# A fused backbone step on one core: the attention's TensorE order written out by hand, with pieces of the gate and q blocks between its products

## The chip, the cores and the metric

The kernel runs on one core of a Trainium2 chip. The core has a matrix engine (TensorE, PE in the profile), a vector engine (DVE), a scalar engine (ACT), a general one (POOL), and a queue engine that issues most transfers (SP). Each works through its own list of instructions in order and waits on semaphores for the others. The metric is the device time of one execution in microseconds (us), lower is better.

## The reference, cut to what matters

One layer of a hybrid backbone over 1024 latent and 128 context tokens, width 1024. One input projection gives the columns of a Fourier mixer, of q (16 heads of 64), k and v (4 kv heads) and of two gates. The part that is changed is the attention with what lies beside it.

```python
def attend_block(qb, k_all, v_all, sink, mask):
    scores = jnp.einsum('btkgd,blkd->bkgtl', qb, k_all,
                        preferred_element_type=jnp.float32) * (HEAD_DIM ** -0.5)
    if mask is not None:
        scores = jnp.where(mask[None, None, None], scores, NEG_INF)
    sink_col = jnp.broadcast_to(sink.astype(jnp.float32).reshape(N_KV_HEADS, Q_PER_KV)[None, :, :, None, None],
                                scores.shape[:-1] + (1,))
    p = jax.nn.softmax(jnp.concatenate([scores, sink_col], axis=-1), axis=-1)[..., :-1]
    return jnp.einsum('bkgtl,blkd->btkgd', p.astype(v_all.dtype), v_all)
...
def merge_branches(u_f, attn_o, g, w_fo, w_ao, w_out):
    gates = jax.nn.sigmoid(g)
    g_f, g_a = gates[..., :D_MODEL], gates[..., D_MODEL:]
    m = g_f * (fourier_mix(u_f) @ w_fo) + g_a * (attn_o @ w_ao)
    return m @ w_out
```

A block of 128 queries sees up to three blocks of 128 latent keys and the 128 cached context keys; the context tokens see only themselves.

## The kernel before

All activations are kept transposed (channels on the 128 partitions). Every matrix product of the input projection is done in three parts with a value split in a high and a low half (`mm3`: high x high, high x low, low x high). The normed input `hs` lies in SBUF (tiles BR and BT) until the last block of q and gate columns is done.

The stages in order: modulation and norm; the Fourier columns and the Fourier mixer, with gate blocks as filler; q of the first kv group; k and v of all nine token tiles (two rounds, PSUM tiles `x`); five gate blocks more (`FILL_KV`); the attention; the Fourier projection `f_unit`; gates, output projection, and the MLP.

A *gate block* (`gate_units`) is 128 gate columns by a third of the tokens (384): 24 products of 384 columns into a PSUM tile `mm`, a copy to `z` by ACT, a store to `z_d`. Three of them share one weight tile, which is loaded (`wraw`), and split by ACT (`whi`, L147) and DVE (`wlo`, L142). A *q block* (`q_units`) has the same 24 products; DVE applies the rotary tables (`qt`, L619 to L625), ACT and DVE split the result, and it is stored to `q_d`. There are 48 gate blocks and 24 q blocks.

The attention runs over 36 *units*, 4 kv groups by 9 query blocks (8 latent ones, one of context). Each has 4 heads and `nb` key blocks (3 at the rims, 4 inside, 1 for context). In `attention_scores`, for each head, two products (L726, L727) put the scores in a PSUM tile `s`, of which there are three. DVE adds the mask, and takes the maximum with the sink logit in the same instruction (L728, result `pt`, maximum `mx`). When a pair of heads has its two maxima, a small DVE instruction multiplies both by -0.125 (L738). Then ACT takes the exponential of each head with that as bias (L740), DVE the reciprocal of the two sums (L748), and POOL scales `pt` (L750). `attention_out` works one unit later: for each pair of heads and two key blocks, PE transposes four 128 x 128 blocks of `pt` into a PSUM tile `ptp` (L769, two buffers), ACT and DVE split it into `ph` and `pl` (L774, L142), and two products of 256 columns per key block (L779, L780) add up the values in a PSUM tile `o`, of which there is one. ACT and DVE add the two halves up (`ot`, `at`) and it is stored to `att_d`. `put_k` transposes the keys of the next group (L805).

Beside the attention run 50 blocks, 18 of q for the next groups and 32 of gates (list `work`, spread over 34 units by `fill`), and 100 steps of the second part of the modulation (`mod_step`: a load `mraw`, two ACT products `mprod`, a POOL sum `macc`, L305 and L307), queued behind POOL's scaling.

What sets the order: the program is traced in the order of the code, and a scheduler at compile time then lays down each engine's list, with the order of the code as priority and a model of its own of how long things take. `issue_after` ties a filler block to the scores of its unit. The order of PE's products within the attention is therefore the scheduler's.

## Time and profile before

| | |
|---|---|
| median of 3 runs (lowest to highest) | 1735.53 us (1731.82 to 1736.85) |
| the profiled execution's own time | 1734.79 us |
| its span, first to last instruction | 1733.0 us |
| granted TensorE clock, mean | 0.986 |
| busy share PE / PEld / DVE / ACT / POOL | 95% / 84% / 67% / 52% / 16% |
| last product of k and v (L235) | 252.1 us |
| first score (L726) / first score of unit 34 of 0 to 35 | 277.0 us / 734.3 us |
| first product of `f_unit` (L880) / of the output projection (L1145) | 741.1 us / 892.5 us |

Times inside the profile are microseconds from the first instruction. PE rows are matrix products, PEld the loads of their stationary operand. Products are pipelined, so a row's duration is longer than the distance to the next one: what a product costs is the distance from start to start. In a group's row stand the busy time and the mean of one instruction in ns, then the engine's idle time just ahead of them, and who ended it.

### The profile page before, as it was taken

To read this page: it belongs to the slowest core of one execution; us is meant where nothing else is said; L and a number is where in the kernel's file an instruction comes from. 1 tells how busy PE (TensorE), PEld (TensorE's weight loads), DVE (VectorE), ACT (ScalarE), POOL (GpSimd) and SP (SyncE) were. 2 spreads that over 40 slices of the span, in tenths; PEclk is the share of its full clock that TensorE was granted. 3 is DMA by queue.
4 is the path that set the end of the run, shared out by engine and by line. 5 is a ranking of instruction groups with operands and counts; after the bars stand their busy time and mean duration, and the time that the engine had idled before them with its cause. 6 is when DMAs were issued, how large, how long until landed. Compare 5 with 4: busy or idle time off the path is not lost.

```text
span 1733.0 us, 25745 instructions
## 1 busy us (share of the span) xinstructions
PE 1640.6 (95%) x8669; PEld 1448.6 (84%) x8669; DVE 1163.2 (67%) x2334; ACT 906.6 (52%) x1826; POOL 272.2 (16%) x368
## 2 busy tenths in 40 slices
PE   6999998789889899999999989999999999999998
PEld 5899887688778888989998788888888888888887
DVE  6653344656856776777856886777776588877764
ACT  7733124566666677766435664444444354444542
POOL 1010013444444445420001210000000200000000
PEclk9999999899999999999999999999999999999999
DMA  8442447324345343249755524454446897556751
GB/s 294 131 145 76 146 150 169 123 77 122 107 107 129 104 120 91 74 141 317 252 174 191 186 98 155 167 171 164 157 145 144 277 384 242 193 186 193 238 176 61
DMA packets 220100, 284.93 MB, mean 164 GB/s; under 512 B 30952, under 2 KB 147624, under 8 KB 219840
## 3 DMA queue, kind: packets, MB, share of 16 engines
q1 hardware_dynamic: 211712, 273.33, 49.5%
q0 software_dynamic: 8256, 9.96, 2.4%
q8 instruction: 68, 1.11, 0.3%
q14 instruction: 64, 0.52, 0.1%
HBM read 205.34 MB, written 77.88 MB: 163 GB/s over the span
## 4 chain that ended last, share of the span: by engine, by line
PE 67%; DVE 8%; DMA 3%; ACT 3%; issue 3%; POOL 1%; SPq 0%; DVEq 0%; ACTq 0%; POOLq 0%
PE x L1711 6%; PE x L1710 6%; PE x L1712 6%; PE x L1314 6%; PE x L1316 6%; PE x L1315 6%; PE mm L195 3%; PE mm L196 3%; PE mm L197 3%; PE x L196 2%; PE x L195 2%; PE x L197 2%; PE ptp L769 2%; DVE pt L728 2%; PE x L1147 1%
## 5 line engine op out<-in xcount | busy, mean ns | idle before, releaser
L142 DVE TENSOR_TENSOR wlo<-wraw,whi 128x1024 fp32r<-128x1024 f32 x108 | 139.3, 1291 | 100.5 <-ACT whi L147 99.5
L147 ACT CAST whi<-wraw 128x1024 fp32r<-128x1024 f32 x106 | 110.8, 1049 | 109.3 <-PE x L235 23.5
L196 PE MATMUL mm<-BR,whi 128*128 128x384 f32 x408 | 140.5, 344 | 0.0
L1711 PE MATMUL x<-BR 128*128 128x512 f32 (+1 forms) x348 | 132.8, 382 | 0.0
L1712 PE MATMUL x<-BR 128*128 128x512 f32 (+1 forms) x348 | 132.4, 382 | 0.0
L1710 PE MATMUL x<-BR 128*128 128x512 f32 (+1 forms) x348 | 131.1, 382 | 0.0
L195 PE MATMUL mm<-BR,whi 128*128 128x384 f32 x360 | 125.2, 348 | 2.4 <-DVE qt L619 2.1
L740 ACT ACTIVATE pt<-pt,mx 128x513 f32<-128x513 f32 (+2 forms) x144 | 94.5, 658 | 58.0 <-DVE mx L738 55.9
L197 PE MATMUL mm<-BR,wlo 128*128 128x384 f32 x360 | 124.0, 344 | 0.0
L750 POOL TENSOR_SCALAR pt<-pt,mx 128x512 f32<-128x512 f32 (+2 forms) x144 | 93.6, 662 | 184.7 <-DVE mx L748 179.0
L728 DVE CUSTOM_DVE_ANT_0 pt<-s,mask,sink 128x512 f32<-128x512 f32 (+2 forms) x144 | 93.1, 673 | 39.3 <-PE ptp L769 33.4
L1683 ACT CAST BR<-aa 128x512 fp32r<-128x512 f32 x80 | 49.7, 621 | 105.2 <-PE x L1711 46.8
L307 POOL TENSOR_TENSOR macc<-macc,mprod 128x512 f32<-128x512 f32 x70 | 92.7, 1325 | 29.9 <-ACT mprod L305 29.8
L142 DVE TENSOR_TENSOR pl<-ptp,ph 128x512 fp32r<-128x512 f32 (+1 forms) x136 | 84.7, 639 | 17.3 <-ACT ph L774 16.0
L726 PE MATMUL s<-kth,qT 128*128 128x512 f32 (+2 forms) x144 | 60.8, 424 | 32.8 <-DVE mx L728 31.0
L769 PE MATMUL ptp<-ident,pt 128*128 128x128 f32 x496 | 74.6, 278 | 10.6 <-DVE pl L142 8.2
L1314 PE MATMUL x<-BR,whi 128*128 128x512 f32 (+2 forms) x204 | 79.2, 388 | 4.1 <-ACT ZR L1338 2.8
L196 PEld LDWEIGHTS mm<-BR,whi 128*128 128x128 f32 x408 | 79.5, 195 | 1.3
L774 ACT CAST ph<-ptp 128x512 fp32r<-128x512 f32 (+1 forms) x136 | 70.9, 547 | 15.1 <-PE ptp L769 12.0
L779 PE MATMUL o<-ph,vg 128*128 128x256 f32 x248 | 68.0, 296 | 10.9 <-DVE at L786 6.2
L305 ACT ACTIVATE mprod<-mraw,siluc 128x256 f32<-128x256 f32 x140 | 63.7, 503 | 27.5 <-POOL macc L307 22.4
L1316 PE MATMUL x<-BR,wlo 128*128 128x512 f32 (+2 forms) x204 | 77.6, 380 | 0.0
(450 smaller groups left out, 4885.6 us busy)
## 6 DMA issues: line engine op xcount, KB each, us to landing
aa<-hr_d SPq DMA_DIRECT2D x108, 256.0 KB
ab<-in_w_ff_dram SPq DMA_DIRECT2D x108, 256.0 KB
hr_d<-ZR SPq DMA_DIRECT2D x104, 256.0 KB
wraw<-in_w_in_dram SPq DMA_DIRECT2D x40, 512.0 KB
wraw<-in_w_ff_dram SPq DMA_DIRECT2D x34, 512.0 KB
mraw<-in_w_ada_dram SPq DMA_DIRECT2D x96, 128.0 KB
wraw<-in_w_out_dram SPq DMA_DIRECT2D x24, 512.0 KB
z_d<-z SPq DMA_DIRECT2D x48, 192.0 KB
```

Source lines behind the costliest of these rows:

```text
L142: eng.tensor_tensor(dst, raw, hi.bitcast(F32), ALU.subtract)
L147: nc.scalar.copy(hi, raw)
L195: nc.tensor.matmul(out, ah, bh, start=start, stop=False)
L196: nc.tensor.matmul(out, ah, bl, start=False, stop=False)
L197: return nc.tensor.matmul(out, al, bh, start=False, stop=stop).ins
L728: nc.vector.tensor_tensor_reduce(out=pt[:, e, :n], in0=sp[:, :n], in1=mask[:, m0 : m0 + n], scale=1.0, scalar=sink8[:, h0 + e : h0 + e + 1 ...
L769: nc.tensor.transpose(pst[:, bi, e, :], pt[:, e, b * P : (b + 1) * P], ident)
L1314: nc.tensor.matmul(po, wh, xh, start=(k == 0 and not cont), stop=False, skip_group_check=cont)
L1316: nc.tensor.matmul(po, wl, xh, start=False, stop=(k == 3), skip_group_check=cont)
L1710: nc.tensor.matmul(ps, xh, bh, start=start, stop=False, skip_group_check=cont)
L1711: nc.tensor.matmul(ps, xh, bl, start=False, stop=False, skip_group_check=cont)
L1712: nc.tensor.matmul(ps, xl, bh, start=False, stop=stop, skip_group_check=cont)
```

## The change

The four parts, as the diff has them:

- **Order.** From unit 0 to 33, PE's list is kept in the order of the code (`manual_schedule` for PE alone); the other engines' lists stay the scheduler's. A q or gate block becomes a generator that hands over after each `mm3` (8 pieces a block). `gap()` is called between the products of the attention and lets so many pieces through that the 440 pieces of 55 blocks are spread evenly by `weight`. A unit then has four scores with a piece or two between them, and after that, for the unit before, transposes and value products in turn: the values of a key block come one key block after its transposes.
- **What stands where.** The five gate blocks behind k and v (`FILL_KV`) go into the attention, and the q blocks of the first group take their place (they stood ahead of k and v).
- **Negative scores.** The DVE instruction that adds the mask multiplies by -0.125 as well and takes the minimum with the negative sink logit; the exponential has scale -1 and that minimum as bias. L738 is gone, and the exponential of a head no longer stands behind the other head of its pair.
- **Four heads at once.** A `ptp` tile holds one key block of four heads (before: two key blocks of two heads); a value product has 512 columns (before: 256), `o` serves four heads, and `ot` and `at` are twice as wide and half as many.

`z` gets three buffers, `ra` and `rb` of k and v one. The diff, cut to what is spoken of:

```diff
-FILL_KV = 5
-FILL_AT = 34
...
+        ZB[0] = 3
...
+        nsink = p1.tile([P, 16], F32, name="nsink")
+        nc.vector.tensor_scalar(nsink, sink_sb, -1.0, None, ALU.mult)
...
+            def piece(j, e):
+                blk = wcols(fetch(ws[e]), KC)
+                ps = mmt()
+                r = slice(j * CH, (j + 1) * CH)
+                v = ps[:, :CH]
+                for k in range(KC):
+                    mm3(v, *blk[k], hs[k][0][:, r], hs[k][1][:, r], k == 0, k == KC - 1)
+                    if k < KC - 1:
+                        yield
...
+        def gate_piece(m, j, w):
+            blk = wcols(fetch(w), KC)
+            ps = mmt()
+            r = slice(j * CH, (j + 1) * CH)
+            for k in range(KC):
+                mm3(ps[:, :CH], *blk[k], hs[k][0][:, r], hs[k][1][:, r], k == 0, k == KC - 1)
+                if k < KC - 1:
+                    yield
+            z = p1.tile([P, CH], F32, tag="z", name=nm("z"), bufs=ZB[0])
+            nc.scalar.copy(z, ps[:, :CH])
+            nc.sync.dma_start(z_d[m][:, j * CH : (j + 1) * CH], z)
...
-            anchor = tok_proj_round(ROUNDS[1], OFF_KV, bankk, evac_kv)
-            filler(FILL_KV, anchor)
+            tok_proj_round(ROUNDS[1], OFF_KV, bankk, evac_kv)
+            for piece in q_pieces(0):
+                for _ in piece:
+                    pass
...
+        def score_head(u, h):
+            g, i, qT = u["g"], u["i"], u["q"]
             k0, nb = KWIN[i]
             n = nb * P
             m0 = MWIN[i] * P
+            pr, e = h // 2, h % 2
+            h0 = g * 4 + pr * 2
+            if e == 0:
+                pt = p1.tile([P, 2, 516], F32, tag="pt", name=nm("pt"), bufs=4)
+                mx = p1.tile([P, 6], F32, tag="mx", name=nm("mx"), bufs=4)
+                u["pts"].append(pt)
+                u["mx"] = mx
+                nc.gpsimd.tensor_copy(pt[:, :, n : n + 1], nsink[:, h0 : h0 + 2].unsqueeze(2))
+            pt, mx = u["pts"][-1], u["mx"]
+            sp = q1.tile([P, 512], F32, tag="s", name=nm("s"), bufs=3)
+            qs = qT[:, h, (i % 3) * P : (i % 3 + 1) * P]
+            nc.tensor.matmul(sp[:, :n], qs, kth[:, k0 * P : k0 * P + n], start=True, stop=False)
+            nc.tensor.matmul(sp[:, :n], qs, ktl[:, k0 * P : k0 * P + n], start=False, stop=True)
+            nc.vector.tensor_tensor_reduce(
+                out=pt[:, e, :n],
+                in0=sp[:, :n],
+                in1=mask[:, m0 : m0 + n],
+                scale=-0.125,
+                scalar=nsink[:, h0 + e : h0 + e + 1],
+                op0=ALU.add,
+                op1=ALU.min,
+                accum_out=mx[:, e : e + 1],
+            )
+            nc.scalar.activation(
+                pt[:, e, : n + 1],
+                pt[:, e, : n + 1],
+                AF.Exp,
+                bias=mx[:, e : e + 1],
+                scale=-1.0,
+                accum_out=mx[:, 2 + e : 3 + e],
+            )
+            if e == 0:
+                return
+            nc.vector.reciprocal(mx[:, 4:6], mx[:, 2:4])
+            for e in range(2):
+                ins = nc.gpsimd.tensor_scalar(
+                    pt[:, e, :n], pt[:, e, :n], mx[:, 4 + e : 5 + e], 1.0, ALU.mult, ALU.mult
+                )
+            if len(msteps) > MOD_B:
+                with tc.issue_after(ins.ins):
+                    mod_step(min(MOD_A[pr], len(msteps) - MOD_B))
+
+        def out_t(u, b):
+            pst = q1.tile([P, 512], F32, tag="ptp", name=nm("ptp"), bufs=2)
+            for h in range(4):
+                nc.tensor.transpose(pst[:, h * P : (h + 1) * P], u["pts"][h // 2][:, h % 2, b * P : (b + 1) * P], ident)
+            ph = p1.tile([P, 512], F32R, tag="ph", name=nm("ph"), bufs=3)
+            pl = p1.tile([P, 512], F32R, tag="pl", name=nm("pl"), bufs=3)
+            nc.scalar.copy(ph, pst)
+            sub(nc.vector, pl, pst, ph)
+            u["p"][b] = ph, pl
+
+        def out_v(u, b):
+            k0, nb = KWIN[u["i"]]
+            if b == 0:
+                u["o"] = q1.tile([P, 512], F32, tag="o", name=nm("o"), bufs=1)
+            po = u["o"]
+            ph, pl = u["p"].pop(b)
+            kb = {"c": 9, "x": 8}.get(KT_ORDER[k0 + b], KT_ORDER[k0 + b])
+            vst = u["v"][:, kb].rearrange("p a d -> p (a d)")
+            nc.tensor.matmul(po, vst, ph, start=(b == 0), stop=False)
+            nc.tensor.matmul(po, vst, pl, start=False, stop=(b == nb - 1))
+            if b < nb - 1:
+                return
+            ot = p1.tile([P, 2, P], F32, tag="ot", name=nm("ot"), bufs=2)
+            at = p1.tile([P, 2, P], F32, tag="at", name=nm("at"), bufs=2)
+            pv = po.rearrange("p (r e t) -> p e r t", r=2, e=2)
+            for e in range(2):
+                top, bot = slice(64 * e, 64 * e + 64), slice(64 - 64 * e, 128 - 64 * e)
+                nc.scalar.copy(ot[top], pv[bot, e])
+                nc.vector.tensor_tensor(at[top], pv[top, e], ot[top], ALU.add)
+            g, i = u["g"], u["i"]
...
-                nc.vector.tensor_scalar(mx[:, 2:4], mx[:, 0:2], -0.125, None, ALU.mult)
...
-                        nc.tensor.matmul(po[:, :256], vst, ph[:, bi, :], start=(b == 0), stop=False)
-                        nc.tensor.matmul(po[:, :256], vst, pl[:, bi, :], start=False, stop=(b == nb - 1))
...
-        def fill(s, after):
-            left = total - min(total, -(-total * s // FILL_AT))
-            with tc.issue_after(after):
-                while len(work) > left:
-                    work.pop(0)()
...
+        def fill_steps():
+            for pc, b, q in pieces_:
+                for w in blocks_[: b + 2]:
+                    fetch(w)
+                for _ in pc:
+                    yield
+                if q is not None:
+                    qdone.add(q)
+                yield
+
+        steps_ = fill_steps()
+
+        def fill_to(x):
+            while done[0] < min(NSUB, round(x)):
+                next(steps_, None)
+                done[0] += 1
+
+        def weight(s):
+            cur = KWIN[units[s][1]][1]
+            prev = KWIN[units[s - 1][1]][1] if s else 0
+            return cur + prev
+
+        NMAN = len(units) - 2
+        wsum = sum(weight(s) for s in range(NMAN))
...
+        man = ExitStack()
+        man.enter_context(tc.manual_schedule(engines={mybir.EngineType.PE}))
+        base, pending = 0.0, None
+        for s in range(NMAN):
+            u = begin(s)
+            nb = KWIN[pending["i"]][1] if pending else 0
+            spots = 4 + (2 * nb + 1 if pending else 0)
+            share = NSUB * weight(s) / wsum
+            seen = [0]
+
+            def gap():
+                seen[0] += 1
+                fill_to(base + share * seen[0] / spots)
+
+            for h in range(4):
+                score_head(u, h)
+                gap()
+            for b in range(nb):
+                out_t(pending, b)
+                gap()
+                if b:
+                    out_v(pending, b - 1)
+                gap()
+            if nb:
+                gap()
+                out_v(pending, nb - 1)
+            base += share
+            fill_to(base)
+            next_keys(*units[s])
+            pending = u
+        fill_to(NSUB)
+        for _ in steps_:
+            pass
+        man.close()
+        for s in range(NMAN, len(units)):
+            u = begin(s)
+            for h in range(4):
+                score_head(u, h)
+            nb = KWIN[pending["i"]][1]
+            for b in range(nb):
+                out_t(pending, b)
+                out_v(pending, b)
+            pending = u
+            if s == NMAN:
+                load_fx()
+            f_unit(NF)```

PE's list at the unit of group 1, query block 4 (unit 13), before. `s` are its scores, `ptp` and `o` the transposes and the values of the unit before it, `mm` a q or gate block.

```order
L726 MATMUL s_4511<-kth,qT_3846 128x512
L727 MATMUL s_4511<-ktl,qT_3846 128x512
L769 MATMUL ptp_4402<-ident,pt_4141 128x128 x4
L726 MATMUL s_4515<-kth,qT_3846 128x512
...
L726 MATMUL s_4536<-kth,qT_3846 128x512
...
L779 MATMUL o_4238<-ph_4244,vg_2722 128x256
L780 MATMUL o_4238<-pl_4245,vg_2722 128x256
...
L769 MATMUL ptp_4415<-ident,pt_4141 128x128 x4
L769 MATMUL ptp_4436<-ident,pt_4170 128x128 x4
L726 MATMUL s_4540<-kth,qT_3846 128x512
L727 MATMUL s_4540<-ktl,qT_3846 128x512
L195 MATMUL mm_4631<-BR,whi_4108 128x384
```

Four scores, three groups of transposes and eight value products stand together there, and the 24 products of a block follow in one piece. The same unit in the changed kernel:

```order
L752 MATMUL s_4234<-kth,qT_3633 128x512
L753 MATMUL s_4234<-ktl,qT_3633 128x512
L193 MATMUL mm_4197<-BR,whi_3479 128x384
...
L752 MATMUL s_4242<-kth,qT_3633 128x512
...
L752 MATMUL s_4279<-kth,qT_3633 128x512
L753 MATMUL s_4279<-ktl,qT_3633 128x512
L193 MATMUL mm_4293<-BR,whi_3828 128x384
...
L786 MATMUL ptp_4297<-ident,pt_4065 128x128 x2
L786 MATMUL ptp_4297<-ident,pt_4099 128x128 x2
L193 MATMUL mm_4293<-BR,whi_3828 128x384
```

A piece of three products (of which only the first is shown) stands between any two scores and behind each group of transposes. In short, with `f` for a piece, `T` and `V` for the four transposes and the two value products of a key block, the unit reads: s f s f s f f s f T f f T f V f T f V f f T f V f f V.

DVE's list from the last score of the same unit on, in the changed kernel; `qt` and `wlo` belong to the q and gate blocks, `pl` is what the value products wait for.

```order
L754 ISA pt_4261,mx_4262<-s_4279,mask,nsink 128x512
...
L140 TENSOR_TENSOR wlo_4376<-wraw_4373,whi_4375 128x1024
L140 TENSOR_TENSOR pl_4303<-ptp_4297,ph_4302 128x512
...
L140 TENSOR_TENSOR pl_4318<-ptp_4312,ph_4317 128x512
L140 TENSOR_TENSOR pl_4336<-ptp_4330,ph_4335 128x512
L633 TENSOR_TENSOR qt_4350<-mm_4293,ropet 128x384
L634 TENSOR_TENSOR qt_4352<-mm_4293,ropet 128x384
L635 TENSOR_TENSOR qt_4275<-qt_4275,qt_4350 128x384
L636 TENSOR_TENSOR qt_4277<-qt_4277,qt_4352 128x384
L140 TENSOR_TENSOR wlo_4658<-wraw_4655,whi_4657 128x1024
L140 TENSOR_TENSOR pl_4370<-ptp_4364,ph_4369 128x512
```

Two weight splits and the evacuation of a q block stand ahead of the first and of the last `pl` of the unit. In the unit after it the scheduler has the four in a row:

```order
L754 ISA pt_4442,mx_4443<-s_4453,mask,nsink 128x512
...
L774 RECIPROCAL mx_4409<-mx_4409 128x2
L774 RECIPROCAL mx_4443<-mx_4443 128x2
L140 TENSOR_TENSOR pl_4482<-ptp_4476,ph_4481 128x512
L140 TENSOR_TENSOR pl_4498<-ptp_4492,ph_4497 128x512
L140 TENSOR_TENSOR pl_4516<-ptp_4510,ph_4515 128x512
L140 TENSOR_TENSOR pl_4533<-ptp_4527,ph_4532 128x512
L811 TENSOR_TENSOR at_4557<-o_4504,ot_4556 64x256
```

Neither list gives a time; it only says what stands behind what.

More of the change, by code (lines that the diff above doesn't have):

```diff
@@ L488, in backbone_kernel @@
         gates = list(gate_units())
+        gate_ids = [(m, j) for m in range(16) for j in range(NJ)]
         def filler(n, after=None):
@@ new lines, in q_pieces, with tile_ @@
+        def q_pieces(g, ws=None):
+            ws = ws or q_weights(g)
+            t = {}
+            tt = nc.vector.tensor_tensor
+            def tile_(n):
+                t[n] = p1.tile([P, CH], F32, tag=f"qt{n}", name=nm("qt"), bufs=1)
+                return t[n]
+            def piece(j, e):
[7 more added lines that the diff above has]
+                        yield
+                c, sn = ropet[:, 0, r], ropet[:, 1, r]
+                if e == 0:
+                    tt(tile_(0), v, c, ALU.mult)
+                    tt(tile_(1), v, sn, ALU.mult)
+                    return
+                tt(tile_(2), v, sn, ALU.mult)
+                tt(tile_(3), v, c, ALU.mult)
+                tt(t[0], t[0], t[2], ALU.subtract)
+                tt(t[1], t[1], t[3], ALU.add)
+                for n in range(2):
+                    hi, lo = t[2 + n].bitcast(F32R), t[n].bitcast(F32R)
+                    nc.scalar.copy(hi, t[n])
+                    sub(nc.vector, lo, t[n], hi)
+                    nc.sync.dma_start(q_d[g, j, n], t[2 + n])
+                    nc.sync.dma_start(q_d[g, j, 2 + n], t[n])
@@ L633, in q_units @@
[L633 to L636 removed]
+                    yield piece(j, e)
+        def gate_piece(m, j, w):
[9 more added lines that the diff above has]
+            nc.sync.dma_start(z_d[m][:, j * CH : (j + 1) * CH], z)
@@ L912, in backbone_kernel @@
             put_k(kv[0][0], q)
-        work, qdone = [], {0: True}
-        def q_last(g, f):
-            f()
-            qdone[g] = True
-        share = -(-len(gates) // NG)
+        blocks_, pieces_ = [], []
+        gate_left = gate_ids[48 - len(gates) :]
+        share = -(-len(gate_left) // NG)
+        gw = {}
         for g in range(NG):
             if g + 1 < NG:
-                fs = list(q_units(g + 1))
-                work += fs[:-1] + [lambda g=g + 1, f=fs[-1]: q_last(g, f)]
-            for _ in range(min(share, len(gates))):
-                work.append(gates.pop(0))
@@ L926, in backbone_kernel @@
-        total = len(work)
-        def fill(s, after):
-            left = total - min(total, -(-total * s // FILL_AT))
-            with tc.issue_after(after):
-                while len(work) > left:
-                    work.pop(0)()
+                ws = q_weights(g + 1)
+                for n, pc in enumerate(q_pieces(g + 1, ws)):
+                    pieces_.append((pc, len(blocks_) + n % 2, g + 1 if n == 5 else None))
+                blocks_ += ws
+            for _ in range(min(share, len(gate_left))):
+                m, j = gate_left.pop(0)
+                if m not in gw:
+                    gw[m] = (OFF_GF + m * P, {}), len(blocks_)
+                    blocks_.append(gw[m][0])
+                pieces_.append((gate_piece(m, j, gw[m][0]), gw[m][1], None))
@@ L961, in backbone_kernel @@
         f_unit(NF2)
-        attention_out(*pending)
+        for b in range(KWIN[8][1]):
+            out_t(pending, b)
+            out_v(pending, b)
     q3 = ctx.enter_context(tc.tile_pool(name="q3", bufs=6, space=PSUM))
```

136 lines of the change are left out of this document (21 added, 115 removed).

## The prediction

> **What bounds the kernel now.** I read the time by stage first, cut where PE's work changes, then who waits for whom in the long stage, then PE's own timeline there.
>
> ```profile
> span 1733.0 us, 25745 instructions
> 171.00:186.00 15.00, 12.92 (x72) 12.61 (x71) 2.72 (x7) 2.84 (x8) 0.84 (x5) 0.96 0.52 189
> 252.00:277.00 25.00, 23.12 (x136) 22.27 (x134) 9.00 (x14) 7.33 (x15) 3.84 (x5) 1.00 1.05 234
> 277.00:734.30 457.30, 402.30 (x2400) 374.31 (x2401) 309.11 (x837) 298.07 (x755) 199.40 (x274) 0.96 0.38 105
> 734.30:892.50 158.20, 155.70 (x926) 150.23 (x925) 123.04 (x263) 85.94 (x186) 13.87 (x29) 0.99 0.70 223
> ```
>
> Columns: length, then busy time of PE, PEld, DVE, ACT and POOL, granted clock, DMA share, GB/s. The attention (fourth row, units 0 to 33) is the place: PE stands idle for 55.0 of 457.3 us, its clock is 0.96, and DVE (309) and ACT (298) are busy for two thirds only. So no engine is full; PE waits on latencies. The row after it is full (155.7 of 158.2).
>
> ```profile
> PEld s L726 <- DVE mx L728: 42.2, 42, 5.1
> PE s L726 <- DVE mx L728: 31.0, 32, 4.8
> ACT pt L740 <- DVE mx L738: 54.2, 36, 4.2
> PE ptp L769 <- DVE pl L142: 8.2, 7, 3.4
> PEld o L780 <- DVE pl L142: 5.2, 10, 1.2
> ACT macc L305 <- DMA mraw<-in_w_ada_dram: 7.5, 5, 3.5
> ```
>
> Most of PE's idle time (31.0) is a score that wants one of the three `s` tiles back from DVE. ACT waits 54.2 us for the small L738. Such a gap costs twice:
>
> ```profile
> 505.00 0.63 PE L769 MATMUL ptp<-ident,pt 128*128 128x128 f32 x4 [1.93 <-DVE pl L142]
> 506.98 0.69 PE L726 MATMUL s<-kth,qT 128*128 128x384 f32 x1 [1.35 <-DVE mx L728]
> ...
> 511.95 0.52 PE L196 MATMUL mm<-BR,whi 128*128 128x384 f32 x1
> 512.27 0.47 PE L197 MATMUL mm<-BR,wlo 128*128 128x384 f32 x1
> ```
>
> After two gaps of 1.93 and 1.35 us the products of 384 columns start 0.32 us apart until 512.27, where 0.17 is usual (below). [...]
>
> **What the same work costs without waits.** Distances from start to start:
>
> ```profile
> 520.86 0.33 PE L195 MATMUL mm<-BR,whi 128*128 128x384 f32 x1
> ...
> 523.80 0.34 PE L197 MATMUL mm<-BT,wlo 128*128 128x384 f32 x1
> ...
> 251.17 0.39 PE L234 MATMUL x<-wlo,BT 128*128 128x512 f32 x1
> 251.40 0.39 PE L235 MATMUL x<-whi,BT 128*128 128x512 f32 x1
> ...
> 517.42 0.28 PE L780 MATMUL o<-pl,vg 128*128 128x256 f32 x1
> 517.54 0.28 PE L779 MATMUL o<-ph,vg 128*128 128x256 f32 x1
> ...
> 525.43 0.87 PE ptp L769 x8
> ```
>
> 17 steps in 2.94 us are 0.173 for 384 columns; 0.228 for 512 (0.23 here); 0.119 for 256 (0.12); 0.109 for a transpose. The counts, by tile, `mm`, `ptp`, `o` and `s` in turn (18 of the `mm` are small ones of the modulation):
>
> ```profile
> 277.00:734.30 457.30, 229.35 (x1194) 214.03 (x1194) 24.43 (x72) 14.79 (x31) 0.96 0.38 105
> 277.00:734.30 457.30, 72.66 (x488) 58.12 (x488) 83.60 (x134) 70.27 (x134) 0.96 0.38 105
> 277.00:734.30 457.30, 77.35 (x445) 65.00 (x445) 36.01 (x126) 32.80 (x126) 0.96 0.38 105
> 277.00:734.30 457.30, 83.49 (x273) 47.29 (x274) 90.80 (x138) 0.00 (x0) 0.96 0.38 105
> ```
>
> 1176 x 0.173 + 2 = 206, 488 x 0.109 = 53, 445 x 0.119 = 53, and 273 scores (192 of 512 columns, the others 384 and 128) 56: together 368 us. So this stage loses 457 - 368 = **89 us**, 55 of them idle and some 18 by the clock (4% of 457). By the same count 252 to 277 holds five blocks (120 x 0.173 = 20.8) and 1.3 us of key transposes and loses 2.9, and at 184.4 the first q block waits for its rotary table:
>
> ```profile
> 184.44 0.44 PE L195 MATMUL mm<-BR,whi 128*128 128x384 f32 x1 [2.08 <-DVE qt L619]
> ```
>
> With the half clock after it, that is 3.9. **Lost before the tail: 96 us.** The work stays the same; what counts is how much of the 96 is lost again.
>
> **The change part by part.**
>
> *Four heads at once* saves PE 2 x 0.119 - 0.228 = 0.01 us a product pair, 0.02 a key block with two pairs: 2.3 us over 116 blocks. The transposes stay as many.
>
> *q of group 0 behind k and v*: the wait for the rotary table goes (3.9), since k and v need no table until their evacuation; the five blocks' cover of the evacuation is replaced by six q blocks (25 us). New there: the first unit reads q back right after it was stored.
>
> ```profile
> 264.87 9.06 DMA qT<-q_d
> ...
> 305.24 4.58 DMA q_d<-qt
> ```
>
> The chain of waits (start, length) has such a load at 9.1 and a store at 4.6 us; the first third is ready 8.3 us into the 25, so it is hidden with some 3 us to spare. I take 0, range 0 to 5.
>
> *Negative scores* remove 68 of these on DVE and let each exponential follow its own minimum:
>
> ```profile
> L738 DVE TENSOR_SCALAR mx<-mx 128x2 f32<-128x2 f32 x68 | 17.5, 258 | 0.3
> L728 DVE CUSTOM_DVE_ANT_0 pt<-s,mask,sink 128x512 f32<-128x512 f32 x96 | 69.2, 746 | 12.2 <-PE ptp L769 11.3
> L142 DVE TENSOR_TENSOR pl<-ptp,ph 128x512 fp32r<-128x512 f32 x103 | 68.9, 686 | 15.0 <-ACT ph L774 14.2
> L142 DVE TENSOR_TENSOR wlo<-wraw,whi 128x1024 fp32r<-128x1024 f32 x15 | 22.9, 1526 | 8.0 <-ACT whi L147 7.0 <-PE ptp L769 0.8
> L619 DVE TENSOR_TENSOR qt<-mm,ropet 128x384 f32<-128x384 f32 x18 | 9.6, 555 | 8.7 <-DMA q_d<-qt 4.7 <-PE mm L197 2.7 <-PE o L780 1.2
> L624 DVE TENSOR_TENSOR qt<-qt,qt 128x384 f32<-128x384 f32 x9 | 7.2, 797 | 0.0
> L740 ACT ACTIVATE pt<-pt,mx 128x513 f32<-128x513 f32 x96 | 68.7, 717 | 41.3 <-DVE mx L738 40.7 <-POOL pt L721 0.4
> L740 ACT ACTIVATION_READ_ACCUMULATOR pt<-pt,mx 128x1 f32 x136 | 25.4, 187 | 0.0
> L774 ACT CAST ph<-ptp 128x512 fp32r<-128x512 f32 x103 | 57.9, 584 | 13.0 <-PE ptp L769 10.4 <-PE o L779 1.6
> ```
>
> DVE's 17.5 us and ACT's waits lie off the sum: neither engine is full. The minimum in place of the maximum is not in the trace; the nearest row is L728 itself, 746 ns, and I take that.
>
> *The order* is the big term. The scores' wait goes: a piece of 3 x 0.173 = 0.52 stands between scores of 0.46, so one comes each 0.98 us where L728 takes 0.75, and there are three tiles. What is late next is `pl`. From a key block's transposes to its values the list leaves 2.0 to 2.5 us (two pieces, other transposes 0.44, a piece, often values 0.46). The chain is the cast (0.58), the subtraction (0.69) and three hand-overs of about 0.15, 1.7 us: enough, if both engines are free. Anything ahead of them in their lists is a wait of PE, and all pieces stand behind it.
>
> I walked four units with these durations. Unit 13, whose DVE list the section on the change shows, is a bad one. From its first score at 0: fourth score at 3.4, DVE busy with `qt` until 4.8, L728 to 5.5, `wlo` (1.53) to 7.2, the first `pl` at 7.9; the second value product wanted it at 7.1: **0.8** lost. After the third `pl`, two of L633's kind (0.56 each, once the block's last product is done at 11.3), two of L635's (0.80), `wlo` again, and the last `pl` ends at 16.2 against 13.8: **2.4**. Unit 14, four `pl` in a row, loses 0.7, since an exponential and a copy stand ahead of the first cast on ACT; units 20 and 21 lose 0.3 and 1.2 (21 evacuates a q block). Mean 1.25 by 34 units is 43; weighed by kind (nine units evacuate a q block, 2.2 each; 25 others 0.5; 19 weight splits, some 0.4) 40. I take **40**. The range is wide: from 10, where queues happen to be clear, to 90, where each of 116 blocks waits 0.8.
>
> *The rest*: first and last units, where nothing is pending or the scheduler's order returns, 3 each; casts behind ACT's waits for the modulation's loads (7.5 before) 4; half clock 5, since the largest gap that I walked, 2.4 us, is shorter than the 3.3 above. [...]
>
> Lost again: 40 + 6 + 4 + 5 = **55**. The span becomes 1733 - 96 - 2 + 55 = 1690. The profiled execution took 1734.79, 1.8 more than its span, and 0.7 less than the median of 1735.5: **1693 us** against that median.
>
> **The rivals.**
>
> *PE runs almost without waits* (the queues of DVE and ACT clear before each `pl`): 15 to 20 us lost in all, 1653 to 1658. For it: DVE (309, less 17.5, and an estimated 20 for the five blocks that move in) and ACT (298 and the same) would be busy for some 310 to 320 of its 400 us. Against it: the list above, where 1.5 to 4 us of other work stand ahead of a `pl`.
>
> *The fixed order gives most of it back*: about 85 lost, 1712 to 1735. That takes a mean of 0.6 to 0.8 us a block.
>
> *Slower: each value product waits behind a full queue.* Place: `ph` on ACT behind an exponential (0.72 and 0.19 for its read of the sum), `pl` on DVE behind an L728 (0.75). The chain is then 1.7 + 0.9 + 0.75 = 3.4 against 2.0 to 2.5 us, 1.1 late, 116 x 1.1 = 128; with the 15 of the rest 143 lost, and the time is 1781. It decides from 0.7 us a block on: 116 x 0.7 + 15 = 96, where nothing is won. The row PEld `o` <- DVE `pl` (10 waits, 5.2 us, half a microsecond each) speaks against it as the rule, and shows that it occurs. [...]
>
> *It doesn't do what it says*: the minimum runs slower than the maximum. At twice 0.75 DVE gets 136 x 0.6 = 80 us more, is nearly full, and PE follows it: about 1740.
>
> **How the numbers follow.** Forecast (1675 to 1711) 0.56, almost no waits 0.17, most given back 0.13, slower 0.10, slow minimum 0.04. 0.3% of the median, about what a measurement can tell from no change, is 5 us: below 1730.3 counts as faster. That takes the forecast, the second and two thirds of the third: 0.82; the same 0.06; slower 0.12. The range reaches from 1653 (the second's end) to 1731 (most of the third); it leaves out some 0.03 below and 0.16 above.
>
> **What would show it.** Right: the scores' wait for DVE falls from 31.0 to under 8 us; the waits of `o` for `pl` and `ph` rise from under 20 to about 40 and become PE's largest; the granted clock of the stage is 0.98 or more; unit 0 to 34 takes some 445 us with 55 blocks in it, and ACT no longer waits for L738. Wrong: PE idle over 80 us in the stage; L728's successor above 0.85 us; a gap of over 5 us ahead of the first score, where q is read back.

## The result, and the profile after

The changed kernel takes **1685.66 us** (median of 4 runs, 1682.73 to 1687.13), the kernel before 1735.59 (1731.82 to 1736.85): a ratio of 0.971, with a 95% interval of 0.969 to 0.973. The forecast was 1693. The profiled execution has a span of 1685.2 us and took 1687.13.

The stages are cut at the same places as before: end of k and v at 225.3, first score at 256.0, first score of unit 34 at 683.9. The attention of the changed kernel between the last two, with the columns as in the prediction:

```profile
256.00:683.90 427.90, 408.53 (x2309) 371.16 (x2308) 289.97 (x705) 295.08 (x693) 194.87 (x274) 0.99 0.44 119
```

It takes 427.9 us where it took 457.3, with five blocks more in it, at a clock of 0.99. I count what was lost as in the prediction: each product by its distance start to start (0.228, 0.174, 0.119 and 0.110 us for 512, 384, 256 and 128 columns), and the stage's length less their sum. Before, the products come to 369.4 us and 87.9 are lost; now to 389.4, and 38.5 are lost. The whole difference of the spans, 1733.0 - 1685.2 = 47.8, is: 49.4 less lost in this stage; 2.4 less work by wider value products; as much lost ahead of it as before, to within 0.2; and 4.3 more lost behind it.

The waits of the same stretch (who waits for whom: us in total, times, longest):

```profile
PEld o L802 <- DVE pl L140: 19.9, 32, 2.3
ACT macc L303 <- DMA mraw<-in_w_ada_dram: 11.9, 7, 4.7
PEld o L801 <- ACT ph L789: 11.8, 10, 5.3
PE o L802 <- DVE pl L140: 8.8, 19, 1.9
PE o L801 <- ACT ph L789: 8.6, 8, 5.0
PE ptp L786 <- POOL pt L776: 0.9, 2, 0.7
PEld s L752 <- DVE mx L754: 0.2, 1, 0.2
```

The scores' wait for DVE, 31.0 us before, is gone (the last row, 0.2 us, is of a weight load; the products themselves have none). What PE still waits for is `pl` and `ph`: 17.4 us as products, 26.4 by the distances from start to start. The longest of these comes from a load. This is the chain of waits (start, length):

```profile
460.02 6.68 DMA mraw<-in_w_ada_dram
466.78 0.70 ACT macc L303 x2
...
470.28 0.48 ACT ph L789
470.80 0.80 PE o L801
```

ACT's list has a product of the modulation ahead of three exponentials (a row `pt` counts each with its read of the sum) and the cast; its load lands late, all of them stand, and PE waits 5.2 us for one value product.

Unit 13, walked in the prediction, shows the ordinary case. DVE's and then PE's timeline at its last key block:

```profile
427.78 0.56 DVE L633 TENSOR_TENSOR qt<-mm,ropet 128x384 f32<-128x384 f32 x1 [0.67 <-PE mm L195]
...
428.72 0.55 DVE L635 TENSOR_TENSOR qt<-qt,qt 128x384 f32<-128x384 f32 x1
429.19 0.55 DVE L636 TENSOR_TENSOR qt<-qt,qt 128x384 f32<-128x384 f32 x1
429.66 1.22 DVE L140 TENSOR_TENSOR wlo<-wraw,whi 128x1024 fp32r<-128x1024 f32 x1
430.79 0.68 DVE L140 TENSOR_TENSOR pl<-ptp,ph 128x512 fp32r<-128x512 f32 x1
```

```profile
427.58 0.60 PE L786 MATMUL ptp<-ident,pt 128*128 128x128 f32 x4
...
430.06 0.40 PE L801 MATMUL o<-ph,vg 128*128 128x512 f32 x1
431.53 0.51 PE L802 MATMUL o<-pl,vg 128*128 128x512 f32 x1 [1.08 <-DVE pl L140]
```

It is the list that was foreseen: evacuation of a q block and a weight split ahead of the last `pl`, and 1.08 us of idle PE (1.25 by the distances) where 2.4 had been worked out.

### The profile page after: what moved, and what is told of

Read it like the earlier page. It is cut to its first block, busy times and chain, and to the rows that moved or that the text cites. A ratio compares the mean times of both kernels' runs of the same rounds, so it can differ in the third digit from the quotient of the medians.

```text
span 1685.2 us, 24900 instructions
## 1 busy us (share of the span) xinstructions
PE 1624.9 (96%) x8421; PEld 1422.9 (84%) x8421; DVE 1137.1 (67%) x2179; ACT 897.0 (53%) x1743; POOL 268.2 (16%) x368
## 3 DMA queue, kind: packets, MB, share of 16 engines
q8 instruction: 66, 1.08, 0.3%
## 4 chain that ended last, share of the span: by engine, by line
PE 64%; DVE 9%; DMA 4%; ACT 4%; issue 3%; POOL 2%; SPq 0%; DVEq 0%; ACTq 0%; POOLq 0%
PE x L1806 6%; PE x L1807 6%; PE x L1805 6%; PE x L1409 6%; PE x L1411 6%; PE x L1410 6%; PE mm L193 3%; PE mm L195 3%; PE mm L194 3%; PE ptp L786 2%; DVE pt L754 2%; PE o L802 2%; PE x L194 1%; PE x L195 1%; PE x L193 1%
## 5 line engine op out<-in xcount | busy, mean ns | idle before, releaser
L140 DVE TENSOR_TENSOR wlo<-wraw,whi 128x1024 fp32r<-128x1024 f32 x109 | 138.4, 1272 | 94.7 <-ACT whi L145 94.7
L193 PE MATMUL mm<-BR,whi 128*128 128x384 f32 x360 | 129.5, 360 | 0.3 <-DVE mods L272 0.3
L140 DVE TENSOR_TENSOR pl<-ptp,ph 128x512 fp32r<-128x512 f32 x124 | 84.7, 687 | 65.2 <-ACT ph L789 64.7
L776 POOL TENSOR_SCALAR pt<-pt,mx 128x512 f32<-128x512 f32 (+2 forms) x144 | 94.7, 670 | 206.3 <-DVE mx L774 204.2
L195 PE MATMUL mm<-BR,wlo 128*128 128x384 f32 x360 | 122.9, 341 | 0.0
L754 DVE CUSTOM_DVE_ANT_0 pt<-s,mask,nsink 128x512 f32<-128x512 f32 (+2 forms) x144 | 94.5, 670 | 14.3 <-PE s L753 11.6
L789 ACT CAST ph<-ptp 128x512 fp32r<-128x512 f32 x124 | 70.9, 578 | 41.7 <-PE ptp L786 37.2
L1409 PE MATMUL x<-BR,whi 128*128 128x512 f32 (+2 forms) x204 | 79.6, 390 | 4.1 <-ACT ZR L1433 2.8
L1410 PE MATMUL x<-BR,whi 128*128 128x512 f32 (+2 forms) x204 | 78.0, 382 | 0.0
L193 PE MATMUL mm<-BT,whi 128*128 128x384 f32 x216 | 77.1, 357 | 0.0
L140 DVE TENSOR_TENSOR BR<-aa,BR 128x512 fp32r<-128x512 f32 x80 | 55.2, 690 | 32.4 <-ACT BR L1778 31.5
L786 PE MATMUL ptp<-ident,pt 128*128 128x128 f32 x496 | 75.1, 274 | 1.8 <-POOL pt L776 0.9
```

The costliest lines, as they stand in the source:

```text
L140: eng.tensor_tensor(dst, raw, hi.bitcast(F32), ALU.subtract)
L193: nc.tensor.matmul(out, ah, bh, start=start, stop=False)
L195: return nc.tensor.matmul(out, al, bh, start=False, stop=stop).ins
L754: nc.vector.tensor_tensor_reduce(out=pt[:, e, :n], in0=sp[:, :n], in1=mask[:, m0 : m0 + n], scale=-0.125, scalar=nsink[:, h0 + e : h0 + e ...
L1409: nc.tensor.matmul(po, wh, xh, start=(k == 0 and not cont), stop=False, skip_group_check=cont)
L1410: nc.tensor.matmul(po, wh, xl, start=False, stop=False, skip_group_check=cont)
```

## The experiments

All times are medians of 4 runs (the fifth row: one run); ratios are against the kernel before on the same chip. "Lost" is the attention's length less its products' own time, as above.

| kernel | time, us | ratio (95%) | attention, us | lost there |
|---|---|---|---|---|
| before | 1735.59 | | 457.3 | 87.9 |
| the change | 1685.66 | 0.971 (0.969 to 0.973) | 427.9 | 38.5 |
| e1: change, order left to the scheduler | 1659.56 | 0.957 (0.954 to 0.961) | 411.0 | 14.5 |
| e2: change, positive maximum | 1704.16 | 0.982 (0.980 to 0.985) | 444.5 | 55.3 |
| e5: change, whole blocks | 1763.53 | (1 run) | 506.5 | 117.8 |
| e3: change, values two key blocks behind | 1685.70 | 0.971 (0.968 to 0.974) | 426.1 | 36.2 |
| g3: change, scores spread | 1698.75 | 0.981 (0.978 to 0.983) | 446.7 | 52.7 |
| h2: change, another written order | 1666.55 | 0.962 (0.960 to 0.964) | 418.4 | 28.2 |
| f1: e1 with positive maximum | 1678.66 | 0.968 (0.966 to 0.970) | 424.5 | 29.6 |
| f2: e1 with whole blocks | 1659.66 | 0.956 (0.954 to 0.958) | 407.5 | 15.3 |
| f3: e1 with values for two heads | 1671.93 | 0.963 (0.961 to 0.965) | 415.2 | 16.5 |
| g5: e1, filling whole behind the last score | 1672.65 | 0.965 (0.964 to 0.967) | 424.2 | 28.8 |
| g1: e1 with q first, five gate blocks behind k and v | 1680.46 | 0.970 (0.968 to 0.972) | 413.4 | 34.8 |
| f4: before with negative scores | 1714.98 | 0.989 (0.987 to 0.990) | 434.2 | 65.4 |

### The written order taken away (e1)

```diff
-        man.enter_context(tc.manual_schedule(engines={mybir.EngineType.PE}))
```

> The changed kernel with TensorE's order in the attention left to the scheduler again; pieces, negative scores, values for four heads and the late q block stay. If the written order brought the gain, the scheduler's list (up to three scores in a row, runs of ten pieces elsewhere) brings back the scores' wait for DVE (over 10 us) and the stage from unit 0 to unit 34 takes over 440 us instead of 427.9: 1700 to 1735 us. If pieces and negative scores brought it, whoever orders them: 1680 to 1692 us.

1659.56: neither theory. The scheduler's order is **26 us faster** than the written one, and the scores' wait for DVE does not come back. PE's waits in the attention of this kernel:

```profile
PE o L801 <- ACT ph L789: 3.5, 1, 3.5
PE s L752 <- DVE mx L754: 1.6, 1, 1.6
...
PE o L802 <- DVE pl L140: 0.3, 1, 0.3
```

So my theory falls twice: the written order was not needed to remove the wait, and against the scheduler's it is itself a loss. What differs shows in PE's timeline of this kernel (the rows left out are pieces, scores, products with `pl`, or belong to other key blocks; the values at 412.63 belong to transposes ahead of these rows):

```profile
403.96 0.60 PE L786 MATMUL ptp<-ident,pt 128*128 128x128 f32 x4
...
405.80 0.60 PE L786 MATMUL ptp<-ident,pt 128*128 128x128 f32 x4
...
412.63 0.39 PE L801 MATMUL o<-ph,vg 128*128 128x512 f32 x1
...
413.09 0.40 PE L801 MATMUL o<-ph,vg 128*128 128x512 f32 x1
...
413.56 0.39 PE L801 MATMUL o<-ph,vg 128*128 128x512 f32 x1
```

The transposes at 403.96 have their values at 413.09, those at 405.80 at 413.56: nine and eight microseconds later, while the written order has 2.5 (427.58 to 430.06). I counted for each key block in the trace the products' own time on PE that stands between its last transpose and its first value product: 2.4 us on average in the changed kernel (nineteen in twenty over 1.5), 6.4 under the scheduler (nineteen in twenty over 3.8). The scheduler often does the transposes of two key blocks close together, puts four to ten pieces behind them, and does the values in bunches of two or three.

### Values later (e3), scores spread (g3)

```diff
             for b in range(nb):
                 out_t(pending, b)
                 gap()
-                if b:
-                    out_v(pending, b - 1)
+                if b > 1:
+                    out_v(pending, b - 2)
                 gap()
...
```

> The changed kernel with the values of a key block two key blocks behind its transposes instead of one (the last of a unit as late as before). If the loss that is left is ph and pl coming late from the queues of ACT and DVE, 15 to 20 of the value products' 26 us of waits go: 1664 to 1672 us. If the queues are simply too long, or three ph and pl tiles too few, so that the wait moves to the transposes or to the next value product: 1682 to 1690 us.

```diff
             for h in range(4):
                 score_head(u, h)
                 gap()
-            for b in range(nb):
-                out_t(pending, b)
-                gap()
-                if b:
-                    out_v(pending, b - 1)
-                gap()
+                if h < nb:
+                    out_t(pending, h)
+                    gap()
+                    if h:
+                        out_v(pending, h - 1)
+                    gap()
```

> The changed kernel, written order kept, with its four scores spread: one score, a piece, one key block's transposes, a piece, the values of the key block before, and so on. If the value products are late because four exponentials (0.91 us each with their read) and the modulation's products queue on ACT ahead of the unit's first casts, their waits fall from 26 to under 12 us: 1662 to 1674 us. If any fixed place is wrong by about as much: 1680 to 1692 us.

Neither gains: 1685.70 and 1698.75. The waits of e3, then those of g3:

```profile
PE ptp L786 <- DVE pl L140: 15.5, 10, 4.7
PE o L802 <- DVE pl L140: 2.1, 5, 0.7
```

```profile
PE ptp L786 <- POOL pt L776: 15.4, 15, 2.5
PE o L802 <- DVE pl L140: 6.2, 14, 1.2
PE o L801 <- DVE at L811: 3.7, 2, 2.7
PE o L801 <- ACT ph L789: 1.9, 5, 0.7
```

In e3 the values hardly wait any more, but the transposes do: with no values between them they follow one another faster, and there are two `ptp` tiles, the older of which is free only when its `pl` is made. In g3 the values' waits fall from 17.4 to 11.8 us (8.1 of them for `ph` and `pl`); by the distances, in which the expectation counts, they fall from 26.4 to some 16, and not to under 12. What undoes even this gain is that the last score now stands late in the unit, its probabilities are scaled late by POOL, and the next unit's first transposes want them: 15.4 us. Each wait was real, and each time the fixed order found the next resource.

### An order with the distance (h2)

```diff
...
-            for b in range(nb):
-                out_t(pending, b)
-                gap()
...
+                if h == 1:
+                    for v in late:
+                        out_v(*v)
+            late = []
+            for b0 in range(0, nb, 2):
+                bl = range(b0, min(nb, b0 + 2))
+                for b in bl:
+                    out_t(pending, b)
+                gap(9 if nb <= 2 else 4 if b0 else 5)
+                late = [(pending, b) for b in bl]
+                if b0 + 2 < nb:
+                    for v in late:
+                        out_v(*v)
...
```

> The changed kernel with another written order: transposes of two key blocks, five or six pieces, the values of both; transposes of the next two, four pieces, and their values only behind the second score of the next unit. The values so stand some 3 to 4.5 us of PE's work behind their transposes instead of 2.4 on average (the scheduler's list has 6.4, and never under 3.5 or so). If that distance is why the written order lost 26 us to the scheduler's, most of it comes back: 1664 to 1674 us, with under 12 us of waits of the values. If a fixed order loses as much wherever things stand, as with two key blocks of distance: 1681 to 1700 us.

1666.55: 19 of the 26 us come back in an order that is written all the same. Waits, and then the timeline of one pair of key blocks:

```profile
PE o L801 <- DVE at L811: 5.8, 5, 2.1
PE o L801 <- ACT ph L789: 3.1, 4, 1.7
PE o L802 <- DVE pl L140: 1.9, 9, 0.2
```

```profile
405.85 1.03 PE L786 MATMUL ptp<-ident,pt 128*128 128x128 f32 x8
...
411.31 0.39 PE L801 MATMUL o<-ph,vg 128*128 128x512 f32 x1
...
411.77 0.39 PE L801 MATMUL o<-ph,vg 128*128 128x512 f32 x1
```

The mean distance is 3.9 us here, and values wait 5.0 us for `ph` and `pl` against 17.4; the new 5.8 is the one `o` tile, which is read out late when the next values follow closely. So a written order need not cost more than 7 us; the other 19 go with a distance of 2.4 us, which is too little for a chain that stands behind ACT's and DVE's other work. The mean distance alone does not decide: by the same count e3 has 3.4 and g3 3.2 us and neither gained, because of the waits shown above, and h2 also does its transposes two key blocks at a time.

### Whole blocks (e5, f2)

```diff
-            while done[0] < min(NSUB, round(x)):
+            while done[0] < min(NSUB, KC * round(x / KC)):
```

Both kernels have this edit; f2 leaves the order to the scheduler as well.

> The changed kernel with the same written order, but each 384-column block issued whole (24 products) where its middle would have stood, so that four scores come in a row and most key blocks have no filling between transposes and values. If the fine interleaving is what the written order is worth, scores wait for DVE again (34 units by about 1 us) and values for pl (about 1.5 us for two key blocks in three, some 110 us): 1760 to 1810 us. If only the fixed order or the amount of filling counts: below 1700 us.

> The scheduler's order, with each 384-column block of filling put into the program whole. Its list still breaks blocks up, into runs of 2 to 10 pieces. If the scheduler's gain over the kernel before comes from filling that it may spread (the kernel before has most blocks as 8 in a row behind the scores), a little is lost: 1662 to 1680 us. If the fine pieces in the program are what it lives on: 1700 us or more, as under the written order (78 us worse).

Under the written order whole blocks cost 78 us (1763.53); under the scheduler nothing (1659.66 against 1659.56). The number lies in the range that the fine interleaving's theory gave for e5, but not by its sum. These are e5's waits:

```profile
PE o L802 <- DVE pl L140: 29.7, 43, 2.8
PE o L801 <- ACT ph L789: 27.4, 33, 7.3
PE s L752 <- DVE mx L754: 5.4, 9, 1.1
```

The scores wait 5.4 us for DVE where 34 were expected, and the values 57.1 where some 110 were. The granted clock, 0.982 over the whole run, takes up to some 32 us (1.8% of its span of 1761.7, an estimate); the rest of the 117.8 that are lost is not located. The scheduler breaks blocks up by itself. The pieces are therefore needed by the written order alone, and are not a gain in themselves.

### Negative scores (e2, f1, f4)

The diff of e2; f1 has the same and leaves the order to the scheduler, and f4 does the reverse in the kernel before:

```diff
-                scale=-0.125,
+                scale=1.0,
...
-                op1=ALU.min,
+                op1=ALU.max,
...
             if e == 0:
                 return
+            nc.vector.tensor_scalar(mx[:, 2:4], mx[:, 0:2], -0.125, None, ALU.mult)
```

> The changed kernel with positive scores again: the maximum, the factor -0.125 as an operation of its own on DVE (68 more of some 0.26 us), both exponentials of a pair behind it. If this work lies off the path, as the prediction has it, within 4 us of the changed kernel: 1682 to 1690 us. If the earlier exponentials are what lets the casts start in time, the value products' waits grow from 26 to over 45 us: 1705 us or more.

> The scheduler's order with the pieces (1659.6 us), with the maximum and its -0.125 back. Under the written order the negative scores were worth 18.5 us, since casts queue on ACT behind exponentials that wait for the other head's score. If that is a matter of a fixed place for the value products, the scheduler, which puts them where it expects pl, loses less: 1662 to 1672 us. If it is the length of the queues whoever orders: 1675 to 1682 us.

> The kernel before with negative scores alone: minimum, no L738, each exponential behind its own minimum. If the 17.5 us of DVE and ACT's 54 us of waits for it lie off the path of the kernel before, as the prediction has it: 1729 to 1739 us. If they hold up casts and subtractions there as they do under the written order: 1712 to 1722 us.

The three agree: **18.5, 19.1 and 19.1 us** (1704.16 against 1685.66, 1678.66 against 1659.56, and 1714.98 against 1734.03, the kernel before on that chip). A row each of f4 and of e2 shows where it acts:

```profile
PE s L726 <- DVE mx L728: 16.9, 22, 5.5
```

```profile
PE o L803 <- ACT ph L791: 12.4, 10, 4.1
PE o L804 <- DVE pl L140: 10.6, 28, 1.1
PE ptp L788 <- POOL pt L778: 4.4, 3, 3.4
```

In the kernel before, the scores' wait for DVE falls from 31.0 to 16.9 us, while the values' wait for the one `o` tile rises from 6.2 to 14.6. In the changed kernel, with the maximum back, waits for ACT, DVE and POOL rise by 3.8, 1.8 and 3.5, and the mean granted clock of the stage falls from 0.99 to 0.98. By the distances the values' waits grow from 26.4 to 35 us, where the second theory of e2 asked for over 45. Engines that are busy two thirds of their time were on the path after all, by the place of this work in their queues. It was not tried how the 19 us divide between the small DVE operation and the exponentials that go earlier.

### What else e1 lives on (g1, f3, g5)

g1 is e1 with the q blocks of group 0 back ahead of k and v, and five gate blocks behind:

```diff
+        for piece in q_pieces(0):
+            for _ in piece:
+                pass
...
-            tok_proj_round(ROUNDS[1], OFF_KV, bankk, evac_kv)
-            for piece in q_pieces(0):
-                for _ in piece:
-                    pass
+            anchor = tok_proj_round(ROUNDS[1], OFF_KV, bankk, evac_kv)
+            filler(5, anchor)
```

> The scheduler's order with the q blocks of group 0 ahead of k and v again and five gate blocks behind them, as in the kernel before. The first q block waits for its rotary table again (3.9 us with the half clock after it in the kernel before): 1662 to 1666 us against 1659.6. If reading q back at once costs as much behind k and v as the table in front: 1657 to 1661 us.

It costs 21 us, not 4. The attention with 50 blocks, and that of e1 with 55:

```profile
273.10:686.50 413.40, 395.38 (x2242) 360.42 (x2240) 287.51 (x701) 292.56 (x690) 206.91 (x282) 0.98 0.48 124
```

```profile
250.10:661.10 411.00, 403.73 (x2349) 376.93 (x2347) 292.07 (x702) 294.39 (x690) 198.88 (x276) 0.99 0.48 127
```

Five blocks of 24 products are 20.9 us of PE's work, and the stage is no longer with them than without: 413.4 and 411.0 us (g1's stretch also holds 13 more products of `f_unit`, 3.0 us). In g1 34.8 us are lost, in e1 14.5. This fits a stage whose length is set by the attention's chain through DVE, ACT and POOL, with the blocks filling what would be waits; f1, which lengthens that chain with the same blocks, takes 424.5. Of the 21 us some 2 are lost ahead of the attention, where the first q block waits for its rotary table again.

f3 is e1 with four value products of 256 columns for each key block:

```diff
+            for r in range(2):
+                c = slice(256 * r, 256 * r + 256)
-            nc.tensor.matmul(po, vst, ph, start=(b == 0), stop=False)
...
```

> The scheduler's order with four products of 256 columns for the values of a key block instead of two of 512. By the distances in the trace of before (0.119 and 0.228) that is 0.02 us a key block, 2 to 3 us over 124: 1661 to 1664 us. If issue slots or weight loads count, 2 more products a block at up to 0.1: over 1670 us.

1671.93, 12 us more than e1 (the intervals of the two ratios don't meet, but nearly). Its profiled execution, the shortest of its runs with a span of 1665.5, shows 4.2 us of it in the attention (415.2 against 411.0): 2.2 of products' own time, as worked out, and 2.0 lost. Another 3.8 of the 7.5 us by which its span exceeds e1's are lost behind the first score of unit 34. So the time lies in the second theory's range, but nothing here shows its mechanism, a price of the products themselves. Where the rest goes stays open.

g5 is e1 with the filling of a unit at its end, whole, and behind the last score, as the kernel before had it:

```diff
...
-            fill_to(base)
+            with tc.issue_after(u["last"].ins):
+                fill_to(KC * round(base / KC))
```

> The scheduler's order with all the filling of a unit as whole blocks at the unit's end and, as in the kernel before, kept behind the unit's last score; its list has runs of 8 to 10 pieces and three or four scores in a row again. If the freedom to put filling between scores is what the scheduler's version gained beside negative scores, the scores' wait for DVE comes back (over 10 us) and the stage loses 40 us or more: 1683 to 1700 us. If the key blocks taken one at a time for four heads, or the new place of the values in the program, brought it: 1658 to 1670 us.

1672.65, between the two theories: 13 us. Its scores wait for DVE again:

```profile
PE s L752 <- DVE mx L754: 10.5, 8, 2.1
```

The stage loses 28.8 us, not 40. So three or four scores in a row do cost a wait for the three `s` tiles, and the freedom to put filling between them removes most of it, whoever orders. Taken out of e1 one at a time, negative scores, the five blocks with the place of q, the free filling and the wider values are worth 19, 21, 13 and 12 us: 65 of the 75 that part e1 from the kernel before, if they add up, which was not tried.

## Why the prediction was right, and where not

The time lies 7 us under the forecast and within its narrow range. Of the signs named, the scores' wait went, the waits of `o` became PE's largest (26 us and not 40), and the clock is 0.99; unit 0 to 34 took 427.9 us and not some 445. The sum held, in part by luck: the gain came largely from other parts of the change than those it was put down to.

**What bounds the kernel: right.** Waits and the half clock of the attention were the loss, and a kernel that loses 14.5 us there (e1) comes to 1659.56, beside the 1653 to 1658 of the rival with almost no waits.

**The order, "the big term": its effect had the wrong sign.** The step "the scores' wait goes: a piece of 0.52 stands between scores" is true of the list, but with the scheduler's list of the same program that wait is 1.6 us as well. Credit for it belongs to negative scores (f4: from 31.0 to 16.9; f1, without them: 5.3) and to filling no longer kept behind the last score (g5, where it is: 10.5). The order's own share is the term that I had as a price, late `pl` and `ph`: 26 us against e1.

**Late values, 40 us: too large.** The mechanism is as told (unit 13), the size 26.4 by distances, 5.2 of it the load of the modulation that I had at 4 apart, so 21 against 40. Unit 13 lost 1.0 and 1.25 us where 0.8 and 2.4 were worked out, unit 14 nothing instead of 0.7, unit 20 nothing instead of 0.3, unit 21 1.1 instead of 1.2. The mean of the four as worked out is 1.35, not 1.25, which makes 46 and not 43; the 40 came from the count by kind. That count was twice too high in both halves: the nine units that evacuate a q block lost 10 us together instead of 20, the other 25 some 11, without the load, instead of 20. In the worst case walked the durations were too long: the weight split took 1.22 us, not 1.53, and L635 0.55, not 0.80 (rows above); the last section has the times of both alone and beside POOL's work. A hand-over, taken at about 0.15, took 0.03 to 0.04 from `ph` to `pl` and 0.05 to 0.06 from `pl` to `o` in the trace of before, and 0.06 in unit 13 (431.47 to 431.53). The rival "slower", each value behind a full queue, asked for 0.7 us a block; 21 by 116 blocks is 0.2.

**Negative scores, 0: wrong.** The step "DVE's 17.5 us and ACT's waits lie off the sum: neither engine is full" failed; they are worth 19 us, in each of three pairs. The minimum itself is no slower than the maximum (744 ns against 746), as assumed:

```profile
L754 DVE CUSTOM_DVE_ANT_0 pt<-s,mask,nsink 128x512 f32<-128x512 f32 x96 | 70.1, 744 | 6.9 <-PE s L753 5.7 <-issue 0.2
```

**q behind k and v, 3.9 us: the term was too small.** The wait for the rotary table went, and reading q back cost nothing. Ahead of the first score one gap stands, and 4.3 us are lost where 2.7 were. PE's timeline there:

```profile
236.51 0.41 PE L832 MATMUL ptp<-ident,kd 128*128 128x128 f32 x2 [2.80 <-ACT rb L708]
```

The key transposes wait for a copy of ACT out of k and v's PSUM tiles. But the five blocks that move into the attention were counted as work that moves and costs the same there. They fill waits: under the scheduler the two moves together are worth 21 us (g1), some 2 of them ahead of the attention. Under the written order this was not tried.

**Four heads at once, 2.3 us:** 2.4 by the products' own time, as said; by the timed runs of f3 more, 12, of which 4.2 lie in the attention and 3.8 behind it in the one traced execution.

**The rest.** Half clock: 5 forecast, 5.9 found, the half of three stretches at half rate (granted clock 0.51, 0.50 and 0.50, from 236.9, 470.8 and 564.6, of 3.4, 5.1 and 3.4 us). What the 5 was set by, a largest gap of 2.4 us as short beside the 1.93 and 1.35 ahead of the half rate in before, no run shows: half rate came behind one gap of 1.89 us, full rate behind one of 2.08 (last section). First and last units, 6: the 4.3 ahead of the first score stand against it, and 4.3 us more than before are lost after the first score of unit 34, which I had not counted. With 38.5 + 4.3 lost from the end of k and v to unit 34 against 55 in the forecast, the changed kernel gained 12 us on it; the 4.3 behind, and the 96 us of before that were 3 too many by the finer count of the whole span, give 7 back. So three errors, negative scores and five blocks at almost nothing and the order as the giver of what they gave, cancelled because all were read out of one quantity, the idle time of PE.

## What to carry to other kernels

Where one engine waits on the latency of others, an operation on an engine that is two thirds busy can be on the path (19 us here), and work moved in as filling can be nearly free (under the scheduler's order here): price both by what waits go, not by their own time. An order written by hand must leave between a producer's request and its consumer the latency of the whole chain behind everything else in those queues; count that distance in the scheduler's own list of the same program before you fix a shorter one (2.4 us lost 26 us to 6.4; 3.9 in pairs lost 7), and look which tile or engine the wait moves to, as in e3 and g3. And when several edits go in together, take each one out by itself, since a sum that comes out right does not say which of them brought it.

## What the runs showed of the hardware

**A subtraction with both inputs in SBUF took longer beside POOL's work.** In the kernel before, a weight split on DVE and its neighbours on POOL:

```profile
363.49 1.28 POOL L307 TENSOR_TENSOR macc<-macc,mprod 128x512 f32<-128x512 f32 x1
363.63 2.21 DVE L142 TENSOR_TENSOR wlo<-wraw,whi 128x1024 fp32r<-128x1024 f32 x1 [1.57 <-ACT whi L147]
364.69 1.20 POOL L721 COPY pt<-sink 128x2 f32<-128x2 f32 x1
```

The same instruction takes 1.22 us where POOL does nothing (429.66 above). Over the whole trace of before, 90 splits with POOL idle took 1.22 us on average and 8 wholly beside POOL's work 1.80 (1.25 to 2.23); subtractions that read PSUM took 0.69 either way. L624 and L625 (L635 and L636 in the changed kernel), whose two inputs lie in SBUF as well, took 0.55 with POOL idle and 0.55 to 2.38 wholly beside its work. And POOL's copy of two elements took 1.20 us beside the split, where the median of such copies is 0.19. The trace does not show what decides: two of the eight splits took hardly longer than alone (1.25 and 1.28). A mean over a stretch (1526 ns for the split, 797 for L624) thus mixes short and long ones. In unit 13 of the changed kernel the short ones held (1.22 and 0.55); in unit 23 a split of 2.30 us stood ahead of a `pl`, and PE waited 1.89 us for it.

**Half rate came after 1.89 us of idle time, and not after 2.08.** In the changed kernel a value product at 563.92 comes after 1.89 us of idle PE, with none in the four microseconds ahead of it. The stretches behind it, with the clock as the third number from the end:

```profile
564.00:565.00 1.00, 1.00 (x5) 0.95 (x6) 1.00 (x3) 0.00 (x0) 0.00 (x0) 0.81 0.57 134
565.00:568.00 3.00, 3.00 (x10) 2.62 (x9) 1.00 (x3) 0.56 (x2) 0.00 (x0) 0.50 1.04 349
```

From 560 to 564 the clock is 1.00. The other two stretches at half rate in this kernel up to the end of the attention come after 2.80 and 5.01 us of idle PE (236.51 and 470.80). In the kernel before, a score at 328.94 comes after 2.08 us of idle PE, and a product at 1008.70 after 2.77; from there to 334 and to 1013 the clock is 1.00. So the runs show no length of a gap that decides. The forecast's 5 us for the half clock was near the 5.9 found.
